# Instance normalisation on one core: an uneven split of one early load over the 16 DMA engines

## The chip, the cores and the metric

## The reference

The input `x` is float32 with 256 x 256 rows of 4096 numbers, 1.07 GB. Each row is brought to mean 0 and variance 1 over its own 4096 numbers:

```
mean = np.mean(x, axis=2, keepdims=True)
var = np.var(x, axis=2, keepdims=True)
return ((x - mean) / np.sqrt(var + eps)).astype(np.float32)
```

Every byte is read once and written once, 2147.5 MB in all.

## The kernel before

The 65,536 rows are cut into 128 tiles of 512 rows. A tile is `[128 partitions, K = 4 rows, 4096]`: each partition holds four neighbouring rows, 64 KB in one piece in SBUF and in HBM. A tile is 8.39 MB. Three tile buffers, `X[0]` to `X[2]`, are used in turn.

For a tile, `vector_tile` (VectorE) sums each of the four rows (L87). `scalar_tile` (ScalarE) squares the row less its mean and sums the squares (L134), and takes the root for two rows at a time (L143). VectorE then forms 1/std (L95) and the negative mean over std (L97), and writes the normalised rows in place (L109); the first three quarters of the last row are done by ScalarE (L148). When the five pieces are done, semaphore `done[s]` lets the store go.

SyncE issues every transfer, all on one queue, and the order is written out by hand. The first tile and the last go in two halves of two rows per partition (L192, `store_half` L178). Then come `load(1, 1)` for the second tile (called at L193, issued at L167), the two half stores of tile 0, `load(2, 2)`, `store(1, 1)`, and then the loop: `store(t)` (issued at L162) and `load(t + 2)` (L167) for each tile. A store waits for the computing of its tile, a load for the store that frees its buffer (`take`, L66 to L68). VectorE waits for a load in `take(V, ld, 16)` at the head of `vector_tile`. So each DMA engine has one list of packets in the order of issue, and in the steady part of the run it alternates between a tile's store and another tile's load.

In the kernel before, every transfer spans all 128 partitions, so that each of the 16 DMA engines gets eight partitions of it, one packet each: 64 KB for whole tiles and 32 KB for half tiles.

## Time and profile before

| what | value |
|---|---|
| time, median of three runs | 4961.14 us (4960.37 to 4961.43) |
| span of the profiled execution | 4959.0 us |
| bytes moved, mean rate | 2147.5 MB, 433 GB/s |
| VectorE busy | 3291.2 us, 66% |
| ScalarE busy | 2407.5 us, 49% |
| median issue to landing of a whole tile's load | 50.3 us |
| median issue to landing of a whole tile's store | 31.6 us |

A line of the profile's page that lists a group reads: line in the kernel, engine, operation, output and input by name, shape and count, then the busy time and the mean of one. "Issue to landing" of a transfer contains the time that it stands behind others in the queue. In an answer by windows, the columns after the window and its length are the busy times of VectorE, ScalarE and GpSimd with their counts, the granted clock of TensorE (not used here), the mean busy share of the DMA engines, and their GB/s. The chain in order of time has start, length, and what ran.

### The profile page before, as it was taken

What the parts mean: (1) busy time and instruction counts of PE and PEld (TensorE: products, weight loads), DVE (VectorE), ACT (ScalarE), POOL (GpSimd) and SP (SyncE); (2) the same over time, 40 slices, a digit from 0 to 9 for tenths busy, and PEclk for the clock granted to TensorE, in tenths of its full rate; (3) what the DMA queues carried; (4) which work ended last, traced back from release to release, by engine and by line L of the source; (5) the groups of instructions that cost most, each with busy time, mean ns of one, the idle gap of its engine ahead of it and who ended that gap; (6) DMA issues with size and microseconds to landing.
All of it is one profiled execution on the core that took longest, in us unless ns stands there. A gap on an engine that the chain in (4) does not pass through costs nothing.

```text
span 4959.0 us, 5426 instructions
## 1 busy us (share of the span) xinstructions
DVE 3291.2 (66%) x1537; ACT 2407.5 (49%) x1412; POOL 0.2 (0%) x4
## 2 busy tenths in 40 slices
DVE  6666666666666666666666666666666666666666
ACT  4455444554445544455444554455444554445544
POOL 0000000000000000000000000000000000000000
DMA  9999999999999999999999999999999999999999
GB/s 422 431 434 434 431 434 435 432 435 435 433 435 434 433 436 433 433 436 433 433 436 433 433 436 433 433 436 433 433 437 432 433 437 432 433 437 432 433 437 408
DMA packets 37298, 2147.52 MB, mean 433 GB/s; under 512 B 4144, under 2 KB 4144, under 8 KB 4144
## 3 DMA queue, kind: packets, MB, share of 16 engines
q1 hardware_dynamic: 37296, 2147.50, 100.0%
q14 instruction: 2, 0.02, 0.0%
HBM read 1073.74 MB, written 1073.74 MB: 433 GB/s over the span
## 4 chain that ended last, share of the span: by engine, by line
DVE 62%; another core or an unknown queue 31%; issue 4%; DMA 2%; ACT 0%; DVEq 0%; ACTq 0%; SPq 0%
DVE total L87 44%; DVE x L109 17%; DMA x<-in_x_dram 1%; DVE nbias L97 1%; DMA out_dram<-x 1%; DVE rstd L95 1%; ACT junk L134 0%; DVEq L68 0%; DVEq L216 0%; ACT L143 0%; ACT std L143 0%; ACTq L68 0%; ACTq L67 0%; SPq L262 0%
## 5 line engine op out<-in xcount | busy, mean ns | idle before, releaser
L87 DVE TENSOR_REDUCE total<-x 128x1 f32<-128x4096 f32 x512 | 2227.1, 4412 | 1591.3 <-DMA x<-in_x_dram 1591.3
L134 ACT ACTIVATE junk<-x,total 128x4096 f32<-128x4096 f32 x512 | 1883.0, 3678 | 2367.0 <-DVE total L87 2367.0
L109 DVE TENSOR_SCALAR x<-x,rstd,nbias 128x4096 f32<-128x4096 f32 (+1 forms) x512 | 1004.1, 2003 | 28.8 <-DVE nbias L97 24.2
L148 ACT ACTIVATE x<-x,nbias,rstd 128x3072 f32<-128x3072 f32 x130 | 383.2, 2948 | 145.5 <-DVEq L68 145.5
L134 ACT ACTIVATION_READ_ACCUMULATOR junk<-x,total 128x1 f32 x512 | 95.4, 186 | 0.0
L143 ACT ACTIVATE std<-ss,eps_tile 128x2 f32<-128x2 f32 x256 | 75.6, 295 | 19.1
L95 DVE RECIPROCAL rstd<-std 128x2 f32<-128x2 f32 x256 | 40.0, 156 | 19.4 <-ACT std L143 19.4
L97 DVE SCALAR_TENSOR_TENSOR nbias<-total,rstd 128x2 f32<-128x2 f32 x256 | 41.1, 161 | 8.9
L134 ACT ACT_TABLE_LOAD x1 | 1.3, 1283 | 1.2 <-DVE eps_tile L213 1.2
L143 ACT ACT_TABLE_LOAD x1 | 1.3, 1283 | 0.1
L213 DVE MEMSET eps_tile<- 128x1 f32 x1 | 0.1, 59 | 1.0 <-SPq L189 1.0
L248 POOL MEMSET const-bfloat16-1.0<- 128x1 bf16 x1 | 0.1, 101 | 0.0
L248 POOL MEMSET const-uint8-127<- 128x1 uint8 x1 | 0.1, 101 | 0.0
L248 POOL MEMSET const-float32-0.0<- 128x1 f32 x1 | 0.1, 98 | 0.2 <-issue 0.2
L248 POOL MEMSET const-float32-1.0<- 128x1 f32 x1 | 0.1, 98 | 0.0
## 6 DMA issues: line engine op xcount, KB each, us to landing
out_dram<-x SPq DMA_DIRECT2D x4, 4096.0 KB, 19.6
x<-in_x_dram SPq DMA_DIRECT2D x2, 4096.0 KB, 16.7
x<-in_x_dram SPq DMA_DIRECT2D x127, 50.3
out_dram<-x SPq DMA_DIRECT2D x126, 31.6
```

The source lines that it names most:

```text
L87: V.reduce_sum(out=total[s][:, r : r + 1], in_=x[:, r, :], axis=AX.X).then_inc(means, 1)
L95: mine(V.reciprocal(out=rstd[s][:, c], in_=std[s][:, c]))
L97: mine(V.scalar_tensor_tensor(out=nbias[s][:, c], in0=total[s][:, c], scalar=-1.0 / d, in1=rstd[s][:, c], op0=ALU.mult, op1=ALU.mult))
L109: V.tensor_scalar(out=x[:, r, f], in0=x[:, r, f], scalar1=rstd[s][:, c], scalar2=nbias[s][:, c], op0=ALU.mult, op1=ALU.add,).then_inc(dn, 1)
L134: mine(A.activation(out=junk, in_=x[:, r, :], func=AF.Square, bias=total[s][:, c], scale=-float(d), accum_out=ss[s][:, c]))
L143: A.activation(out=std[s][:, c], in_=ss[s][:, c], func=AF.Sqrt, bias=eps_tile, scale=1.0 / d**3).then_inc(stds, 1)
L148: A.activation(out=x[:, last, :Q], in_=x[:, last, :Q], func=AF.Identity, bias=nbias[s][:, c], scale=rstd[s][:, c]).then_inc(dn, 1)
L213: V.memset(eps_tile, eps).then_inc(ready, 1)
L248: nc = _bacc.Bacc("TRN2", target_bir_lowering=False, num_devices=1)
```

## The change

One transfer, the load of the second tile, is replaced by ten. The first brings rows 0 to 2 of each partition (48 KB per partition) for all 128 partitions. The fourth row (16 KB per partition, a quarter of the tile) is brought by eight transfers of eight partitions each, which cover partitions 0 to 63, and by one transfer of the 64 other partitions. It is meant to place the eight small transfers on the same eight DMA engines, which then get eight packets of 16 KB more than the other eight: an offset between two halves of the DMA engines, early in the run. All else is as before: later loads and stores, computing and buffers. The ten transfers count on one semaphore of their own, `extra`, and VectorE waits for ten times 16 before it starts on this tile.

```diff
+    extra = nc.alloc_semaphore("extra")
...
-    def vector_tile(s, r0=0, k=K, ld=None, dn=None):
+    def vector_tile(s, r0=0, k=K, ld=None, dn=None, count=16):
...
-            take(V, ld, 16)
+            take(V, ld, count)
...
-        load(1, 1, wait=False)
+        S.dma_start(out=X[1][:, : K - 1, :], in_=x_t[1][:, : K - 1, :]).then_inc(extra, 16)
+        for p in range(0, P // 2, 8):
+            S.dma_start(out=X[1][p : p + 8, K - 1, :], in_=x_t[1][p : p + 8, K - 1, :]).then_inc(extra, 16)
+        S.dma_start(out=X[1][P // 2 :, K - 1, :], in_=x_t[1][P // 2 :, K - 1, :]).then_inc(extra, 16)
...
-        vector_tile(1)
+        vector_tile(1, ld=extra, count=10 * 16)
```

## The prediction

> **What bounds the kernel now.** I read the page from the top: the busy lines, the DMA row of the slices, and the queues.

> ```profile
> DVE 3291.2 (66%) x1537; ACT 2407.5 (49%) x1412; POOL 0.2 (0%) x4
> DMA  9999999999999999999999999999999999999999
> DMA packets 37298, 2147.52 MB, mean 433 GB/s; under 512 B 4144, under 2 KB 4144, under 8 KB 4144
> q1 hardware_dynamic: 37296, 2147.50, 100.0%
> ```

> The reader is to see that no engine is near full, while the 16 DMA engines are busy in every slice. One queue carries all the bytes, so every engine works through its own list in issue order: a tile's load, the store before it, the next load. The chain of waits names VectorE for 62% only because the reduction happens to be the last event before each landing; the waits of VectorE say the opposite:

> ```profile
> DVE total L87 <- DMA x<-in_x_dram: 1591.3, 126, 13.5
> ```

> VectorE waits 1591 us for loads, and the queue never waits for anything that would leave the DMA engines empty. At 500.42 the store of one tile is issued while the load issued before it still has 12.3 us to go (it lands at 512.7). So transfers bound the time, and what matters is when the slowest of the 16 engines is through its list.

> Next I asked whether all engines keep pace. The chain in order of time shows when each tile's reduction starts, which is when the slowest engine has landed that tile:

> ```profile
> 122.08 17.40 DVE total L87 x4
> 161.53 17.40 DVE total L87 x4
> 200.87 17.40 DVE total L87 x4
> 240.08 17.40 DVE total L87 x4
> 318.22 17.40 DVE total L87 x4
> 356.89 17.40 DVE total L87 x4
> ...
> 1094.27 17.40 DVE total L87 x4
> ...
> 4339.85 17.40 DVE total L87 x4
> ...
> 4803.53 17.40 DVE total L87 x4
> ```

> From 4339.85 to 4803.53 there are 12 tiles: 38.64 us each. The first ones take longer: 39.45, 39.34, 39.21, then 78.14 for two. From 122.08 to 1094.27 there are 25 tiles, 972.19 us, where 25 x 38.64 is 966.0: 6.2 us lost. The tile before 122.08 (its reduction starts at 82.55 in the timeline) took 39.53, 0.9 more: **7.1 us lost by about 1094 us, and none after**.

> The trace's packet records and the records of the 16 completion increments of each transfer explain it. A 64 KB packet takes 2.418 us, loads and stores alike, from the 1st to the 99th percentile within 0.01 us. The exceptions lie almost all before 1000 us: at 38.9 us 16 packets took 3.65 to 4.11 us, and later the last packets of a load took 2.5 to 3.4 us on some engines, while other engines had already gone over to the next store. So the engines drift apart: the 16 increments of one transfer land within 0.5 us of each other at 43.5 us, within 3.2 at 240, 4.6 at 435, 6.9 at 765 and 7.25 at 1152. There it stays. In that state nine to ten engines are close together, the first seven within 0.35 us, and five or six trail; between the groups is a gap of some 4 us, which a single drifting engine crosses. Windows at the end show the price:

> ```profile
> 4938.00:4950.00 12.00, 2.56 (x2) 2.39 (x1) 0.00 (x0) 1.00 0.96 412
> 4950.00:4959.00 9.00, 0.00 (x0) 0.00 (x0) 0.00 (x0) 1.00 0.33 142
> ```

> In the last 9 us the DMA share is 0.33: the leaders are done at 4951.3, and the trailing engines run on until 4957.6. The span is set by the trailing group.

> [...] 16 x 65536 bytes in 2.418 us is 433.7 GB/s. Packets are already at that rate with loads alone, stores alone, or both in flight[...].

> **The change part by part.**

> *Issue.* One issue at L167 (0.42 us in the timeline, at 1.88) becomes ten. Ten by 0.42 is 4.2 us, so SyncE is through at about 6.1. Queued behind is the wait of the first half store, which ended at 31.50. The engines have 19.4 us of tile 0 ahead of them (16 packets of 32 KB by 1.21 us). Hidden behind both: 0.

> *Wait.* VectorE waits for 160 on the new semaphore where it waited for 16. In before it comes to tile 1 at 48.17, and tile 1 had landed at 43.52. The trailing engines now land it 2.4 us later, about 45.9, still ahead of 48.17. Behind that wait is the rest of VectorE's work, and ScalarE waits for its sums. Cost 0.

> *Bytes per engine.* Before: eight packets of 64 KB per engine, 512 KB. [...] The difference is 128 KB, two packets of 64 KB or 4.84 us; against the even split it is plus and minus 64 KB, **plus and minus 2.42 us**. Nothing evens it out later[...].

> *Small packets.* Twelve more packets at most for an engine, and nine more completion writes (9 ns each in the packet records). Pauses of 0.17 to 0.21 us between packets occur in places; if each of the eight little transfers brought one, that would be 1.7 us. The trace has no 16 KB packet. I take 0.3 us, with 0 and 1.7 as ends.

> *The spread.* [...] What the slowest loses in before is 7.1 us. How much of this remains is not shown by before; its bounds are 0 and 7.1. For a small rest speaks that the settled state, a gap of some 4 us between two groups, loses nothing, and that seven engines in step lose nothing. For a larger rest speaks that the trailing engines were still losing while the whole spread was 4.6 to 6.9 us (packets of 2.9 to 3.4 us between 468 and 626 us), and that nobody has shown that eight trailing engines in step are at peace. I take 0.6.

> Sum for the slowest engine: +2.4 - 7.1 + 0.6 + 0.3 = -3.8 us. The last tile's stores follow its landing by the same computing as before, and those engines never run dry: the store of a tile is issued about 27 us after it lands, and they have 38.6 us of work in that time. 4961.1 - 3.8 = **4957.3 us**, -0.08%.

> **The rivals.**

> 1. *The losses come again in full.* If they are the property of certain engines, or of how the eight in the rear sort themselves out, the 7.1 us stay and the extra bytes come on top: +2.4 + 0.3, **4963.8 us**. For it: losses at a spread of 4.6 us. Against it: 11 of the 16 engines lost hardly anything after 435 us, so being ahead or behind seems to decide.
> 2. *The conflict never settles* (slower). Leaders can be ahead by at most about 11.6 us (38.64 - 27 us) before their list is empty and they wait for the next issue. If the rear group needs 4.84 plus a further 7.3, that is 12.1: the leaders are held back and the loss repeats. At 0.27 us per tile, the growth between 435 us (4.6) and 765 us (6.9, 8.5 tiles later), 126 tiles cost 34 us: **4995 us**. Against it: the settled state in before has packets of 2.418 us for 3800 us, in all mixtures of loads and stores, and one engine crosses the gap without loss.
> 3. *Faster by over 0.2%* (9.9 us). Even with no loss on any engine, and 1.6 us gained on the slow packets at 38.9, the slowest gains 7.1 + 1.6 - 2.4 = 6.3: **4954.8 us**. A gain of 9.9 would need quicker packets[...].

> **How the numbers follow.** Forecast 0.62; rival 1 0.28; rival 2 0.06; rival 3 at its limit of 4954.8 0.04, of which 0.02 for something beyond that limit. The range goes from 4954.0 (just past the limit of rival 3) to 4965.2: rival 1 with the 1.7 us of pauses in place of 0.3, which is 4961.1 + 2.4 + 1.7. Only rival 2 and the unforeseen lie outside. Faster by over 0.2% 0.02, within 0.2% 0.92, slower 0.06.

> **What would show it.** Right: the 16 increments of tile 1's load land in two groups, some 4.8 us apart; tile periods are 38.64 from about the fifth tile on, with fewer packets over 2.44 us; the final spread is still 5 to 8 us. If the spread is right and the periods still run at 39.3 for ten tiles, rival 1 holds. If periods stay over 38.7 after 1100 us, rival 2 holds. My reading of the placement is wrong if tile 1's increments stay within 1 us of each other.

## The result, and the profile after

| | before | after |
|---|---|---|
| time, median of four runs | 4960.78 us | 5026.57 us (5021.6 to 5028.55) |
| ratio | | 1.0131, 95% interval 1.0116 to 1.0146 |
| span of the profiled execution | 4959.0 us | 5025.8 us |

The change costs 66 us: 5026.6 us, where 4957.3 us was forecast and the range ended at 4965.2. The page of the changed kernel still shows DMA engines that are never idle for long and an unchanged VectorE:

```profile
DVE 3291.5 (65%) x1537; ACT 2407.5 (48%) x1412; POOL 0.2 (0%) x4
DMA  9999999999999999999999999999999999999999
DMA packets 37506, 2147.52 MB, mean 427 GB/s; under 512 B 4224, under 2 KB 4224, under 8 KB 4224
q1 hardware_dynamic: 37504, 2147.50, 99.9%
```

The busy share says nothing here: an engine whose packet takes 3.0 us in place of 2.42 is as busy as before. The rate tells it, 427 GB/s for 433, with the same bytes. The waits say the same: VectorE stands 66 us longer waiting for loads.

```profile
DVE total L88 <- DMA x<-in_x_dram: 1657.1, 127, 13.9
```

Where did it go? In the chain in order of time (start, length, what ran), the start of a tile's reduction is again the landing of the tile on the slowest engine.

```profile
96.57 17.40 DVE total L88 x4
135.57 17.40 DVE total L88 x4
174.58 17.40 DVE total L88 x4
...
1073.96 17.40 DVE total L88 x4
1112.62 17.40 DVE total L88 x4
...
4869.53 17.40 DVE total L88 x4
4946.85 17.40 DVE total L88 x4
```

Two things are to be seen. Tile 2 starts at 96.57, where it was 82.55: **14.0 us are gone before the loop begins**. From 96.57 to 4946.85 there are 124 tiles, 39.12 us each; a period like 38.66 (1073.96 to 1112.62) comes singly. In before the period settled at 38.64. So **a loss of almost half a microsecond a tile lasts to the end**; from tile 1's landing to the last tile's it makes 52.3 us more than in before, whose own early loss of 7 us is in that comparison. 14.4 (tile 1's landing, 57.9 for 43.5) and 52.3 make 66.7 of the 66.8 us between the two spans.

The first part lies in the load that was changed. Windows of after, with the columns as before (DMA share and GB/s at the end):

```profile
24.00:36.00 12.00, 7.98 (x6) 6.65 (x6) 0.00 (x0) 1.00 0.96 414
37.00:44.00 7.00, 3.13 (x1) 6.34 (x4) 0.00 (x0) 1.00 1.03 143
82.50:84.50 2.00, 1.55 (x2) 1.39 (x1) 0.00 (x0) 1.00 0.61 262
2000.00:2500.00 500.00, 325.64 (x148) 236.45 (x139) 0.00 (x0) 1.00 1.00 428
```

From 37 to 44 us, when the 16 KB packets run, all engines are busy and move 143 GB/s. In the packet records most of these packets take 1.9 to 2.0 us, for 0.61 in the quick stretch of the run spread below: the small ones to partitions 0 to 63, and also the leading engines' own four to partitions 64 to 127 that run beside them. The trailing engines' own four, at the end, take about 1.3 us. The engines with eight packets more come out 12.1 to 13.4 us behind in the next store, not 4.84. Then the late tile 1 makes itself felt: VectorE waits for it,

```profile
58.02 17.40 DVE L88 TENSOR_REDUCE total<-x 128x1 f32<-128x4096 f32 x4 [9.68 <-DMA x<-in_x_dram]
```

so `store(1, 1)` is issued at 84.13 for 74.27 (start, length, engine and line, what was issued; before first):

```profile
74.27 0.33 SPq L162 DMA_DIRECT2D out_dram<-x  x1
84.13 0.33 SPq L163 DMA_DIRECT2D out_dram<-x  x1
```

The leading engines' list is empty by then (share 0.61 from 82.5 to 84.5).

The second part is in the packet records: 2198 packets of 64 KB over 2.44 us, for 192 in before, spread evenly from 100 us to the end. In a tile around 490 us, the eight trailing engines have packets of 2.75 to 3.3 us at the end of their load, and the eight leaders of 3.0 us near the end of their store. From tile 3 on, the spread between the first and the last engine's landing stays at 10.2 to 11.7 us.

### The profile page after: what moved, and what is told of

The parts are those of the page before. It is cut to its first block, busy times and chain, and to the rows that moved or that the text cites. A ratio compares the mean times of both kernels' runs of the same rounds, so it can differ in the third digit from the quotient of the medians.

```text
span 5025.8 us, 5435 instructions
## 1 busy us (share of the span) xinstructions
DVE 3291.5 (65%) x1537; ACT 2407.5 (48%) x1412; POOL 0.2 (0%) x4
## 2 busy tenths in 40 slices
DMA  9999999999999999999999999999999999999999
DMA packets 37506, 2147.52 MB, mean 427 GB/s; under 512 B 4224, under 2 KB 4224, under 8 KB 4224
## 3 DMA queue, kind: packets, MB, share of 16 engines
q1 hardware_dynamic: 37504, 2147.50, 99.9%
## 4 chain that ended last, share of the span: by engine, by line
DVE 62%; another core or an unknown queue 32%; issue 4%; DMA 1%; ACT 0%; DVEq 0%; SPq 0%; ACTq 0%
DVE total L88 44%; DVE x L110 17%; DMA x<-in_x_dram 1%; DVE nbias L98 1%; DVE rstd L96 1%; ACT junk L135 0%; DVEq L69 0%; DVEq L220 0%; ACT std L144 0%; ACT L144 0%; SPq L179 0%; ACTq L69 0%; ACTq L68 0%; SPq L266 0%
## 5 line engine op out<-in xcount | busy, mean ns | idle before, releaser
L96 DVE RECIPROCAL rstd<-std 128x2 f32<-128x2 f32 x256 | 40.2, 157 | 19.4 <-ACT std L144 19.4
```

The costliest lines, as they stand in the source:

```text
L96: mine(V.reciprocal(out=rstd[s][:, c], in_=std[s][:, c]))
```

## The experiments

Three theories were set against each other for the second part. Theory 1: the size of the offset decides, over some 10 us it does harm. Theory 2: eight engines against eight collide for good at any offset. Theory 3, formed after the first four runs: what decides is the **lead**, the work that the leading engines still have in their list when the next store and load are issued. In before, a store is issued 12.3 us ahead of the landing of the load in progress on the last engine; what the leaders are ahead comes off this, so in after they have 0.7 to 2.5 us left.

### How many small transfers: small2, small4, small6

Each brings the first 16, 32 or 48 partitions' fourth rows by 2, 4 or 6 small transfers, the rest by one (six are shown).

```diff
-        for p in range(0, P // 2, 8):
+        for p in range(0, 48, 8):
...
-        S.dma_start(out=X[1][P // 2 :, K - 1, :], in_=x_t[1][P // 2 :, K - 1, :]).then_inc(extra, 16)
+        S.dma_start(out=X[1][48 :, K - 1, :], in_=x_t[1][48 :, K - 1, :]).then_inc(extra, 16)
...
-        vector_tile(1, ld=extra, count=10 * 16)
+        vector_tile(1, ld=extra, count=8 * 16)
```

> Two small transfers in place of eight, the other 112 partitions' fourth rows in one transfer. Theory 1 (the size of the offset decides: up to about 7 us is harmless, 10 us is not): the increments of tile 1 and the next stores land in two groups some 3 to 5 us apart (a small transfer holds an engine about 1.95 us), the loss per tile ends within some 25 tiles, spread at the end about 7 us, time 4957 to 4963 us. Theory 2 (eight engines against eight collide for good at any offset): the loss of 0.4 to 0.5 us a tile stays, 5010 to 5025 us.

Measured: 4974.61 us (4968.06 to 4985.84), ratio 1.0016 (0.9992 to 1.0039); the two groups of engines 1.2 to 1.8 us apart in the next store.

> Four small transfers. Theory 1: groups 6 to 8 us apart, at the edge of the harmless size, so a time of 4960 to 4970 us with a constant tile period of 38.64 us from early on. Theory 2: 5010 to 5025 us.

Measured: 4971.16 us, ratio 1.0019 (1.0012 to 1.0027); groups 2.3 to 3.0 us apart.

> Six small transfers. Theory 1: groups 9 to 11 us apart, the loss of about 0.4 us a tile stays to the end, 5005 to 5025 us. Theory 2: 5010 to 5025 us too. If the time is below 4975 us, an offset of 9 to 11 us alone is not harmful, and theory 1 has its threshold wrong or is wrong.

Measured: 4985.33 us, ratio 1.0049 (1.0032 to 1.0065); groups 4.6 to 5.4 us apart, which is the offset that the change was meant to have.

Theory 2 is out: small6 has two groups of eight and loses nothing for a long time. The chain of small6 shows three stretches:

```profile
206.80 17.40 DVE total L88 x4
...
670.46 17.40 DVE total L88 x4
...
1096.05 17.40 DVE total L88 x4
...
3108.96 17.40 DVE total L88 x4
...
3418.61 17.40 DVE total L88 x4
3458.27 17.40 DVE total L88 x4
3496.97 17.40 DVE total L88 x4
3536.45 17.40 DVE total L88 x4
```

From 206.80 to 670.46, twelve tiles of 38.64 us: lossless, long before before is. From 1096.05 to 3108.96, 52 tiles of 38.71. From 3418 on, periods of 39.66, 38.70, 39.48: the loss of after. The landings show what the 0.07 us is: from 1444 to 2606 us, 30 tiles, the last of the 16 increments of a load falls 2.2 us further behind the fifteenth, while the other 15 keep their distances within 0.3 us. So by its landings one engine needs 38.71 us a tile, 2.419 us for each of its 16 packets, where the others need 38.64, or 2.415. That engine is the last, so all wait for it, and the spread grows by its 0.07 us a tile from 6.3 to 10 us. Then the third stretch sets in. Before has such an engine too (0.05 us a tile between 1400 and 4100 us), but it starts among the leaders and crosses the gap without being last, as the prediction saw without asking what it would cost elsewhere. Small4 and small2 run through the same drift, and small2 reaches the third stretch at about 4000 us. Theory 1's times for small2 and small4 were too low, because the drift was not in them. Its time for small6, 5005 to 5025 us, was too high. In all three the groups stood closer together than expected.

### Whole partitions for the small transfers: big2

```diff
+        for p in range(0, 16, 8):
+            S.dma_start(out=X[1][p : p + 8, :, :], in_=x_t[1][p : p + 8, :, :]).then_inc(extra, 16)
+        S.dma_start(out=X[1][16:, :, :], in_=x_t[1][16:, :, :]).then_inc(extra, 16)
```

(these three in place of the ten transfers of the changed kernel)

> The same two packets of 64 KB more on eight engines as the change meant, but as two transfers of eight whole partitions (64 KB packets), and the other 112 partitions in one. If a single packet costs its engine the larger of about 2 us and its bytes, the groups are 4.8 us apart; if it costs 1.4 us on top of its bytes, 7.6 us. Theory 1: 4955 to 4965 us either way. Theory 2: 5010 to 5025 us.

Measured: 4990.78 us, ratio 1.0057 (1.0041 to 1.0074). A miss for both: the first two 64 KB packets of each engine took 7.8 to 9.3 us and most of the others of this tile 4.8 to 5.5, and tile 1 landed at 69.9 us for 43.5. So a fixed cost per transfer is not what makes the small packets slow: four times the bytes took some four times as long. From tile 5 to about 1650 us this kernel, with a spread of 7.9 us, ran at 38.63 to 38.64.

### Where the small packets clash: spread, spread_sbuf

```diff
-        for p in range(0, P // 2, 8):
-            S.dma_start(out=X[1][p : p + 8, K - 1, :], in_=x_t[1][p : p + 8, K - 1, :]).then_inc(extra, 16)
+        for g in range(0, P // 2, 32):
+            for p in range(g, g + 4):
+                S.dma_start(out=X[1][p : p + 29 : 4, K - 1, :], in_=x_t[1][p : p + 29 : 4, K - 1, :]).then_inc(extra, 16)
```

(spread_sbuf reads `x_t[1][q : q + 8, ...]` with `q = g + 8 * (p - g)`, and writes as spread does)

> The change, with each of the eight small transfers on partitions four apart (p, p+4, ... p+28) in place of eight neighbours; the same bytes on the same engines. If eight neighbouring partitions get in each other's way (in the on-chip memory or in HBM) and so cost 1.95 us a packet, the packets now take 0.6 to 0.7 us, the two groups stand 4 to 6 us apart at the next stores, and the time is 4956 to 4972 us. If a transfer with one packet per engine has a fixed cost, packets stay at 1.9 us, the groups 12 us apart, and the time 5020 to 5030 us.

Measured: 4998.75 us, ratio 1.0074 (1.0057 to 1.0091).

> As spread, but read from eight neighbouring blocks of HBM and written to partitions four apart: 64 fourth rows of tile 1 land in other partitions of their group of 32, so those output rows are another row's. If the clash is where it is written (SBUF), the small packets take 0.6 to 0.7 us and the groups stand 4 to 6 us apart. If it is where it is read (HBM), 1.9 us and 12 us.

Measured: 5003.43 us, one run. In both, the small packets take 1.3 us while the leaders' own 16 KB packets run beside them and 0.61 us after, the trailing engines' own four then 1.2 to 1.3 us again, and the groups stand 7.0 to 7.6 us apart. Windows of spread:

```profile
37.00:41.00 4.00, 3.10 (x1) 3.33 (x3) 0.00 (x0) 1.00 0.99 205
42.00:44.00 2.00, 0.00 (x0) 2.00 (x2) 0.00 (x0) 1.00 0.98 418
500.00:1300.00 800.00, 527.81 (x245) 382.82 (x224) 0.00 (x0) 1.00 1.00 435
2000.00:2500.00 500.00, 327.18 (x156) 236.90 (x141) 0.00 (x0) 1.00 1.00 430
```

From 42 to 44 us the small packets run at 418 GB/s. Reading eight neighbouring blocks of HBM makes no difference, writing to partitions four apart does: the clash is where eight neighbouring partitions are written (1.9 to 2.0 us a packet in after, 1.3 and then 0.61 here). Why they clash there is not shown, nor why the leaders' packets, to other partitions, took 2.0 us beside them. What holds the packets at 1.3 us from 37 to 41 us, and again at the end, is open too; in before the 16 packets from 38.9 us on were slow as well (3.65 to 4.11 us for 2.42).

The last two windows show the other half of the story again: with a spread of 8.3 to 9.8 us the loop runs at 435 GB/s, and from about 1650 us, when the drift has brought the spread over 10, at 430.

### Issuing later or earlier: late, early

Late is the kernel before, with one more sum of a row in each tile of the loop:

```diff
+        if late:
+            V.reduce_sum(out=spare, in_=x[:, r0, :], axis=AX.X)
```

> The kernel before, with one more row sum of 4.4 us (written to a spare column) in every tile of the loop, so that every store and load of the loop is issued 4.4 us later. The leading engines, 7.3 us ahead in the settled state, then have 0.6 us of work left at the issue in place of 5.0. Theory 1 (the offset itself decides): settled period still 38.64 us, 4960 to 4966 us. Theory 3 (an issue that comes just in time for the leaders makes the slow packets): period 39.0 or more for as long as the spread is over 7 us, 4985 to 5015 us.

Measured: 5005.11 us as the median of 13 runs, ratio 1.0063 (1.0037 to 1.0089). The runs fall in two heaps: four at 4962.75 to 4963.49, nine at 4999.63 to 5014.15. The profiled execution (5002.6 us) is of the upper one. From 1000 us on its spread is 5.7 to 7.2 us, harmless in before, and its loop runs nearly at the rate of after (the first two lines are of before, the others of late):

```profile
1000.00:2500.00 1500.00, 996.68 (x465) 724.68 (x425) 0.00 (x0) 1.00 1.00 434
3800.00:4700.00 900.00, 603.23 (x279) 438.44 (x256) 0.00 (x0) 1.00 1.00 435
1000.00:2500.00 1500.00, 1152.19 (x503) 716.69 (x422) 0.00 (x0) 1.00 1.00 430
3800.00:4700.00 900.00, 693.07 (x300) 432.77 (x254) 0.00 (x0) 1.00 1.00 429
```

Long times of this size are not tied to a change alone: of 78 executions of the kernel before that were timed beside the experiments, two took 5001.48 and 5008.73 us, all others 4960 to 4965. No trace of these two exists, so it is not shown that they are the same loss.

Early is the changed kernel with less computing in the loop, the mean and variance of half of each row:

```diff
-            V.reduce_sum(out=total[s][:, r : r + 1], in_=x[:, r, :], axis=AX.X).then_inc(means, 1)
+            V.reduce_sum(out=total[s][:, r : r + 1], in_=x[:, r, :h], axis=AX.X).then_inc(means, 1)
...
+                vector_tile((L0 + j) % BUFS, h=d // 2)
```

> The changed kernel, with the mean and variance of every tile of the loop taken over the first half of each row only, so that stores and loads are issued some 9 us earlier. Theory 1: the offset of 10 to 12 us is still there, and so are the slow packets, 5015 to 5035 us. Theory 3: slow packets vanish, period 38.64 to 38.71 us, 4972 to 4985 us.

Measured: 4990.56 us, ratio 1.0054 (1.0038 to 1.0071), 6 us over the upper end that theory 3 gave. Its windows:

```profile
1000.00:2500.00 1500.00, 660.46 (x462) 452.70 (x422) 0.00 (x0) 1.00 1.00 434
3800.00:4700.00 900.00, 396.02 (x277) 271.83 (x254) 0.00 (x0) 1.00 1.00 430
```

With a spread of 14.5 to 19 us the loop runs at 434 GB/s from 1000 to 2500, and falls to 430 only when the drift has carried the spread to 19. So theory 1 is wrong: 6.5 us does harm when the issue is late, 17 us none beyond the drift when it is early. Between these runs it is the lead that decides. From the records of landings and issues, for each tile from the twelfth on (the lead is from the issue of a store to the first landing of the load in progress, the period is that of the tile after):

| run | lead of the first engine 2.5 us or more | lead under 2 us |
|---|---|---|
| before | 113 tiles, spread 7.2, period 38.66 | none |
| late | 7 tiles, spread 4.8, period 38.83 | 60 tiles, spread 6.6, period 39.23 |
| small6 | 56 tiles, spread 7.8, period 38.70 | 33 tiles, spread 11.1, period 39.09 |
| after | none | 75 tiles, spread 11.2, period 39.31 |
| early | 47 tiles, spread 15.7, period 38.75 | 53 tiles, spread 19.4, period 38.90 |

Spreads from 6.6 to 19.4 us go with the loss. The tiles between the two columns, with a lead of 2.0 to 2.5 us, are followed by 38.79 us in late, 38.80 in small6, 38.73 in after and 38.87 in early, so the edge lies near 2 us of lead, a little less than one packet of 2.42 us. In its first tiles after lost at 1.9 to 2.5 us of lead too. Within one run lead and period hang together (a tile that lands late leaves more lead), so the weight lies on the comparison between runs. (The 38.83 of late is from early tiles, where the build-up that the prediction described still runs.)

### More lead with the whole computation: half_after, half_before, half_small6, early_before

```diff
-        take(S, done[s], K + 1)
-        S.dma_start(out=rows_of(out_t, t), in_=X[s][:, :, :]).then_inc(stored[s], 16)
+        S.wait_ge(done[s], half)
+        S.dma_start(out=rows_of(out_t, t, 0, half), in_=X[s][:, :half, :]).then_inc(stored[s], 16)
+        take(S, done[s], K + 1)
+        S.dma_start(out=rows_of(out_t, t, half, K), in_=X[s][:, half:, :]).then_inc(stored[s], 16)
```

(the loads then wait for 32)

> The changed kernel, with every store of the loop issued in two halves, the first as soon as its two rows are done (some 4 us earlier), each half with its 9.7 us of work per engine. Theory 3 (slow packets come when an issue finds the leaders with less than about one packet, 2.4 us, left): the leaders, 10 to 13 us ahead, always have 5 us or more left, the period is 38.64 to 38.71 us, and of the time only the start's 14 us and a drift of up to 8 us remain, 4970 to 4985 us. Theory 1 (the offset): period 39.1, 5015 to 5030 us.

Measured: 4987.78 us as the median of six, 4978.76 to 4991.06 for four of them, and two at 5019 and 5024; theory 3 gave 4970 to 4985. The profiled execution (4978.8 us) has a spread of 12.6 to 14.0 us and no after-like stretch:

```profile
1000.00:2500.00 1500.00, 992.87 (x466) 721.38 (x424) 0.00 (x0) 1.00 1.00 433
3800.00:4700.00 900.00, 592.03 (x277) 431.08 (x254) 0.00 (x0) 1.00 1.00 433
```

From 330 us on the period is 38.66 to 38.76, at a larger spread than that of after. That is theory 3 again, with the computing of after unchanged, so that less computing, as in early, is not needed for it. But its lead ahead of the first half store was 1.9 to 3.5 us, not the 5 us expected, at the edge. That the two long runs fell over it is not shown: no trace of them exists, and half_before, which comes next, has two long ones as well.

> The kernel before with the same half stores, as the control. Both theories: the settled period stays 38.64 us; the losses of the first 25 tiles may differ with the smaller packets; 4955 to 4965 us.

Measured: 4971.07 us as the median of 13, with two at 4986.50 and 5013.71, ratio 1.0029 (1.0014 to 1.0043): half stores are no gain by themselves, the settled period is 38.68 us, and the build-up of the spread goes on longer (38.88 us a tile from 825 to 1214).

> Six small transfers, with half stores. Without them this kernel ran at 38.71 us per tile until the spread was 10 us, and at 39.1 from there. Theory 3: 38.64 to 38.71 to the end, 4964 to 4974 us. Theory 1: 4980 to 4990 us as without the halves.

Measured: 4976.89 us, ratio 1.0031 (1.002 to 1.0043), 8 us under small6 and 3 over the upper end expected; period 38.68 to 38.75 until 4350 us, 38.86 in the next ten tiles. In those ten the lead ahead of the first half store was over 7 us, and so it was in half_before while its spread built up: a short lead is one condition for a loss, not the only one.

> The kernel before, with the mean and variance of the loop's tiles over the first half of each row, as in the run early: stores and loads issued some 9 us sooner. Theory 3: the leaders already had 5 us left when settled, so more lead brings nothing, period 38.64 us, 4957 to 4964 us. If the build-up of the first 25 tiles is gone as well, it was a matter of the lead too, and the time is 4953 to 4957 us.

Measured: 4969.81 us, ratio 1.0013 (1.0005 to 1.0022), a miss. Here the build-up ends at a spread of 4.4 us, and from 821 to 1594 the period is 38.64; but then one engine, 0.13 us a tile slower than the others by its landings, becomes the last and drags the period to 38.77 for the rest. The drift needs no uneven split. No version beat the kernel before.

## Why the prediction was wrong

*What bounds the kernel, and the build-up in before:* right. Transfers bound it (DMA share 1.00 at 434 GB/s from 1000 to 2500 us in before), and an offset from the start does take the build-up away: small6, big2 and spread reach 38.64 us per tile within some five tiles.

*Issue:* right. The eight small issues took 2.98 us together, and SyncE was through at 5.9 us (6.1 predicted).

*Bytes per engine, and small packets:* the placement was right, engines in two groups of eight. The eight small transfers land in eight increments each, the first of them at 39.16 to 39.86 us, and the 16 increments of the next store come as eight at 54.06 to 55.41 and eight at 66.79 to 67.50. That is 576 KB of tile 1 for each engine of the rear and 448 KB for each leader; the numbers of the engines are in no record. The size was wrong, in the term "I take 0.3 us, with 0 and 1.7 as ends". Tile 1 landed 14.4 us late; with 2.4 for the bytes, that term was 12.0. The step took a packet's time from transfers that span all partitions, and asked about pauses between packets, not whether eight packets go to the same place. At the measured 1.95 us, eight of them are 15.6 us, for 4.84.

*Wait:* "Cost 0" failed with it. VectorE waited until 58.0 us for tile 1, where it was free at 48.3, and the next store was issued 9.9 us later.

*The spread:* this is the step that cost most. "I take 0.6" was for what remains of 7.1 us when eight engines trail from tile 1 on, in place of drifting there in 25 tiles, -6.5 us in the sum; in its place the loop lost 52.3 us more than before did. By the prediction's own sign, periods over 38.7 after 1100 us, rival 2 holds. Rival 2 named the direction and nearly the mechanism, with 0.06 for its chance: the rear group 12.1 us back, against a limit of 11.6. Its rate was 0.27 us a tile, the measured one 0.48. Its reason was too strict: the list need not be empty. Some 2 to 2.5 us in it at the issue is little enough, so the limit in before is an estimated 10 us (12.3 less these), and after lives above it at 10.2 to 11.7.

*The limit of rival 3:* that no packet gets quicker was the author's estimate from before, whose quickest 64 KB packet took 2.418 us; in after it was 2.415. As a rule it is not shown.

*Would it have held at the intended offset?* No. Small6 is that offset, and took 4985.3 us. Its tile 1 landed 7.7 us late, at 51.2; for the rest the missing piece is the one slower engine. The prediction used it ("one engine crosses the gap without loss") as evidence of peace, when it was a drift that costs 0.07 us a tile once this engine is the last, and uses up the lead.

What stays open: why packets far from the issue (7 us later on the trailing engines) slow down when the lead was short, which engine is the slower one and why (the packet records do not number the engines), why late and half_after come out in two heaps, and what made the two long executions of before. Taking the slower engine out of the rear was not tried.

## What to carry to other kernels

Transfers that are cut up should be checked for which partitions they touch at the same moment, not only for bytes per engine: while eight engines wrote eight neighbouring partitions, all 16 ran at a third of their rate (143 GB/s for 433, after from 37 to 44 us). In a loop that the DMA engines bound, ask how much work the *earliest* engine still has when the next transfer is issued; below about 2 us, less than one packet (2.42 us), this loop lost 0.3 to 0.7 us a tile, in after to the end, while every engine showed as busy. And a small difference between engines that costs nothing now (0.05 us a tile in before) can be on the path after a change of who is last (0.07 in small6, 0.13 in early_before).

## What the runs showed of the hardware

- Each of the 259 transfers of before landed in 16 increments. From each transfer to the next in the order of issue, the first increment, the second and so on to the 16th all come later.
- With two transfers of eight partitions and one of 112 (big2), the first two 64 KB packets of all 16 engines took 7.8 to 9.3 us and most of the others 4.8 to 5.5, for 2.42 in transfers of 128 partitions.
- One of the 16 engines loses 0.05 us (before), 0.07 (small6) or 0.13 (early_before) on the others in every tile of 38.64 us, for thousands of microseconds.
- A leading engine with under 2 us of work left at the issue goes with packets of 2.7 to 3.3 us (2.42 otherwise) on trailing and leading engines, some 7 and 18 us later, in after at 475 us.
